# Attention stage of a trunk layer: 20 of 32 maximum shifts on GpSimd, and another order of the stage's works

## The chip, the cores and the metric

The kernel runs on one core of one Trainium2 chip. A core has five engines with a queue each, and each queue is worked off in order: PE (TensorE, matmuls; PEld is its weight load, which overlaps the matmuls), DVE (VectorE), ACT (ScalarE), POOL (GpSimd) and SP (SyncE, which here only issues DMAs). The metric is the time of one execution on the device in microseconds (us); less is better. Line numbers (L1123) are those of the kernel's file.

## The reference

One layer of a transformer trunk is computed for 128 context tokens and 512 latent tokens, with shared weights: a normalised and modulated projection `w_in`, attention beside a short gated convolution, an output projection, and a convolutional feed-forward part. The change lies in the attention, of which this is the core:

```python
q = rms_norm(q.reshape(B, N, N_HEADS, HEAD_DIM), p["q_norm"])       # 16 heads of 64
k = rms_norm(k.reshape(B, N, N_KV_HEADS, HEAD_DIM), p["k_norm"])    # 4 key heads
...
s = jnp.einsum('bqkgd,btkd->bkgqt', qblk, k).astype(jnp.float32) * scale
p = jax.nn.softmax(s, axis=-1).astype(v.dtype)
return jnp.einsum('bkgqt,btkd->bqkgd', p, v)
```

Context tokens attend to 128 keys without positions; latent tokens are rotated by two-dimensional positions and attend to 640 keys, of which 128 come from a cache.

## The kernel before, in words

**Values in two parts.** fp32 values are split into a high part (fp32r, by a copy on ACT) and a low part (value minus high part, a subtraction on DVE or POOL), and each product is three matmuls: high·high, low·high, high·low.

**The stage.** The attention stage begins when the projections of keys and values are done and ends before the attention's output projection (L235 to L237). It has 4 key heads g; for each it goes through 5 tiles t of 128 query tokens (tile 0 is the context). Each tile holds four query heads in two pairs. The 36 steps are numbered n = 9g + i: i = 0 is the context tile with both pairs at once, and i = 1 to 8 are tiles 1 to 4 with one pair each. These last are the 32 *blocks*; each treats two heads, h = 0 and h = 1.

**Before a block: a query tile.** `q{g}{t}.0` to `.3` are four quarters of its projection on PE (L709, 6 matmuls each). DVE rotates (`rot`: L849 and L850, into the tiles X and QF), DVE or POOL adds the two (`add`, L870), ACT squares (L872), DVE sums (L874), POOL takes the power -1/2 (`factor`, L877), POOL or DVE multiplies by it (`norm`, L892). PE turns the tile over (`turn`, L1034), and ACT and DVE split it (`hi`, `lo`: L1036, L1038). The key tiles go a similar way (`k{t}`: L849, L850, L870, L877, L882, L921, L927, L930). The values are scaled to an fp16 pair (`v scale`, L975; `v hi`, L981; `v lo`, L984).

**A block n.** `s{n}`: PE computes the scores of both heads (L1073, 12 matmuls), each head into one of three PSUM areas of two banks. `max{n}.h`: DVE takes the negated maximum over 640 keys (L1120). `shift{n}`: for h = 1 alone a constant is added to it (L1123, one number per partition). `exp{n}.h`: ACT (L1128), with the sum accumulated by a second instruction. `P1`: ACT rounds to fp16 (L1134). `P2`: the rest, again fp16; for h = 0 always on DVE (L1141), for h = 1 by L1139 on POOL or DVE. `T{n}.h`: SP issues a transposing DMA (L1145). `pv{n}`: PE multiplies with the values (L1162, L1170). Then `R`, `O`, `AH`, `AL` (L1182 to L1192) scale and split the output.

**Two ways for P2 of the second head.** Where `POOL_WAY` has a 1 for a block, the exponential goes to a buffer E in SBUF and POOL computes P2 from it; the score's PSUM area is free after the exponential. Where it has a 0, the exponential stays in PSUM and DVE computes P2. Before, blocks 28, 34 and 35 have a 0.

**What sets the order.** Nothing is scheduled in the stage while the kernel runs or is built: `PLAN` is a list of 944 items, each the number of a work, a letter (a or b: on which of its possible engines it is done) and digits (which free buffer or PSUM area it takes). `follow(PLAN)` issues them in that order. So each engine's queue holds its works in the order of the list, and a work waits there for its inputs, and for the last users of the buffers that it takes. Loads of weights (`load`) and their splits (`hi 10` to `hi 18`, `lo 10` to `lo 18`: L826, L831, two halves of 512 columns for each low part) are works of the list as well. A weight's low half that is not ready holds the projection quarters that use it.

The lines of a work that can be done by two engines look like this, here the addition of a query tile:

```python
last = also(work(f"{name} add", "POOL", lambda: add(G), [rot], orooms + [zt]), "DVE", lambda: add(V))
```

Of the kernel before, what the change touches and what calls it, by code (L numbers as in the profile page):

```python
# [18 lines left out]
ALU = mybir.AluOpType  # L19
# [31 lines left out]
67a0 44a0 12a00 203a 24a1 137a 34a2 68a 25a 13a 0a 32a11 131a 2a1 69a 11a 26a 6a 3a 41a 33b 70a 14a1 35a 51a2 4a 1a3 79a1 53a4  # L51
71a0 15a 21a 80a 36a 5b0 31a 72a2 81a 45a 52a3 7a 16a 37b1 82a 22a12 92a2 46a 85a1 73a 8a0 23b 83a10 17a2 54a3 9a 86a 132a 38a1
10a 27a3 42a01 18a0 39a 93a 55a 19a 43a 40a 28a4 74a 60b2 94a 29a 59b3 95a 87a 75b 20a 105a3 98a0 84a 30a 76a1 106a 88a 77a0 99a
78a 107a 100a 58b4 56a0 47b4 65a 347a2 57a 134b 61a 96a22 48a1 63a 348a 108a 97a 49a 118a0 349a 101a 109a01 119a 133b 50a 89a2
102a1 120a 62a 90a1 209a 111a2 351a1 91a 110a 121a 112a 138a 66a 113a 359a10 352a 124a1 103a2 114a 122a10 204a 353a5 365a 140b
115a4 135a0 116a3 366a 104a 367a0 139b 136a 117a 350a 360a 368a0 373a20 123a 275a 125a 361a 64a 126a 141a 362a4 379a 205b 142a
380a 371a 363a 381a1 354a1 369a 143a2 364a0 382a2 374a 391a10 355a2 144a0 356a 383a 375a 151a0 370a1 145a 397a 357a 152a 376a1
146a 398a 385a 384a2 392a 399a0 153a 377a 147a 393a 154a 358a 206b 405a02 394a3 378a3 155a01 400a4 395a 127a 148a1 157a2 411a
401a 149a0 128a3 372a0 396a4 129a1 412a 158a 413a1 130a 159a 406a 414a0 423a12 403a 402a5 150a 407a 415a 164a1 429a 408a2 165a
156a 430a 281a 409a 431a0 166a 416a0 160a 424a 432a1 167a 417a 425a 433a 437a02 168a20 426a3 435a 386a 170a1 443a 169a 410a1  # L60
444a 427a 177a1 387a2 445a1 388a 178a 438a 389a 428a2 446a4 455a12 390a 171a 439a 447a 404a0 456a 440a0 434a3 449a 457a 441a
172a 418a 461a 458a2 173a 161a2 442a4 419a1 179a 459a 162a2 180a 163a 462a 420a 463a0 469a10 448a5 181a10 464a3 467a 182a 487a2
470a 183a0 421a 465a 190a1 460a0 488a 471a 191a 475a 472a1 192a 422a 210a 184a 466a1 174a0 473a 193a 185a 175a3 489a 176a 476a
186a 194a02 450a0 211a 436a 212a 477a1 474a4 490a 195a 478a0 481a 499a10 196a2 907a 479a 451a1 197a 207a1 491a4 505a 276a 208a
198a 506a 480a5 452a 507a0 492a 213a 199a 500a 453a 513a20 508a2 493a2 454a 278b 501a 468a0 514a 509a 502a3 519a 515a 214a 503a
277b 510a3 516a1 482a 520a 215a2 521a1 517a 187a3 504a0 483a0 511a 525a 531a02 188a1 484a 522a0 189a 518a1 200a3 216a1 523a 537a
485a 494a1 201a0 486a 538a 217a 223a0 495a2 202a 524a4 218a 539a0 496a 224a 532a 497a 219a 540a4 545a12 498a 533a 911a 541a
220a1 551a 534a2 225a 221a2 552a 226a 535a 542a5 553a1 546a 554a3 563a02 227a11 547a 555a 536a2 222a 548a1 557a 512a1 569a 229a0
228a 570a 549a 571a0 526a 556a0 564a 572a0 577a12 543a 230a 527a0 573a 565a 528a 550a3 236a0 583a 529a 566a4 231a 237a 575a 584a
578a 585a1 238a 574a1 567a 232a 586a2 239a 530a 579a 587a 595a20 240a02 568a4 580a3 589a 544a1 242a2 601a 241a 602a 596a 558a  # L70
603a0 588a2 581a 597a 233a0 243a 609a01 234a3 607a 244a 559a1 582a5 235a 604a1 560a 249a0 610a 245a 561a 598a0 250a 562a 605a
611a 599a 246a1 251a 247a1 615a 600a0 612a4 627a2 616a 248a 617a1 252a 628a 606a3 618a2 590a1 621a 613a 255a1 619a 629a 256a
576a 253a20 614a2 257a 254b 639a10 591a2 620a5 630a 631a3 592a 258a 262a0 640a 593a 263a 594a 641a 645a 264a 282a 646a 632a 265a
647a0 633a1 283a 279a1 266a11 284b 642a0 280a 648a1 643a 653a20 267a 915a 268a0 651a 908a 644a4 269a 649a 608a0 654a 659a 655a
622a 270a 909a 650a0 656a4 259a3 660a 271a 661a1 285a 657a 910b 260a0 286a 665a 623a0 658a3 261a 662a2 272a2 624a 671a21 287a0
625a 663a 288a2 626a 273a2 289a 634a1 919a 677a 290a 664a2 295a0 678a 635a2 672a 679a0 291a 296a 274a 673a 636a 685a10 637a 683a
674a3 638a 297a 691a 680a0 298a 681a 692a 675a 693a1 292a1 299a21 676a5 694a1 703a20 686a 300a 301a1 293a3 302a 666a0 695a 687a
682a1 709a 688a4 697a 294a 652a 710a 303a 704a 696a2 711a0 689a 308a1 667a0 304a 705a 668a 717a01 690a3 669a 715a 712a2 670a
# [10 lines left out]
880a0 885a 934a 840a 856a0 841a 895a 886a5 896a 842a 935a2 897a 890a 898a1 936a 891a 899a 937a 892a4 901a 900a2 938a 943a 893a  # L89
939a 894a4 940a 870a 888a1 871a2 872a 902a 873a 874a 941a 903a1 904a 942a 905a 906a  # L90
"""
POOL_WAY = "11111111111111111111111101111100"


def rope_tables():
# [17 lines left out]
def trunk_layer(ctx, tc, x_prompt, x_sample, cache_k, cache_v, c, c_ctx, w_ada, b_ada, g_pre1, g_post1, g_pre2,  # L113
# [597 lines left out]
    SHIFT = 15  # L711
# [35 lines left out]
    with tc.tile_pool(name="att", bufs=1) as at:  # L747
# [305 lines left out]
        for n, (g, t, pi) in enumerate(steps):  # L1053
# [52 lines left out]
            else:  # L1106
                pts[n], exs = [], []
                for h in hs:
# [16 lines left out]
                    if h:  # L1125
                        mx = work(f"shift{n}", "DVE", shifted, [mx])
# [1398 lines left out]
```

## Time and profile before

| | us |
|---|---|
| median of three runs (lowest, highest) | 1075.21 (1074.77, 1075.44) |
| the profiled execution's own time | 1074.79 |
| its span | 1073.0 |
| of it the attention stage, about | 55 to 229 |

The granted clock of TensorE is full (0.999) all through. A row of a timeline or of the chain gives the start and the duration in us, the engine, the line, the operation, out<-in by names, and in brackets how long the engine had been idle and what released it. A row of groups gives the count, the busy time in us and the mean of one in ns, then the idle time ahead of them. Rows of windows give the busy time of each engine within a stretch. A busy PE is not a PE at its peak: matmuls are pipelined and their ends modelled.

### The profile page before, as it was taken

The numbers are of one execution on the slowest core, as the hardware profiler recorded it, in microseconds if no ns is written. First come the engines' busy times: TensorE is split into PE (matmuls) and PEld (weight loads), VectorE is DVE, ScalarE is ACT, GpSimd is POOL, SyncE is SP. The second block draws the span as 40 slices with busy tenths as digits, with TensorE's granted clock in tenths as the row PEclk, the third lists the DMA queues.
The fourth block names the chain that finished last, engine by engine and source line by source line (L and its number), as shares of the span: only waits on it lengthen the run. The fifth ranks groups of instructions, "written<-read, shape, count | busy, mean of one in ns | idle before, by whom it ended". The sixth has DMA issues, their size and how long they took to land.

```text
span 1073.0 us, 20652 instructions
## 1 busy us (share of the span) xinstructions
PE 1056.8 (98%) x8216; PEld 995.4 (93%) x8216; DVE 899.9 (84%) x1379; ACT 598.4 (56%) x1057; POOL 133.1 (12%) x162
## 2 busy tenths in 40 slices
PE   8999999999999999999999999999999999999997
PEld 6788898899999999999998789999999999999996
DVE  5699999865498999896599678889999988989897
ACT  5478999942344544445322366645555555546673
POOL 1087676500000000000000020000000000000001
PEclk9999999999999999999999999999999999999999
DMA  9829999962244333223668634434544534436873
GB/s 320 256 82 175 190 168 187 191 147 60 75 123 124 93 103 94 79 79 99 189 188 253 198 131 129 121 116 136 166 131 152 150 122 131 152 116 219 277 275 115
DMA packets 243197, 164.02 MB, mean 153 GB/s; under 512 B 94874, under 2 KB 216214, under 8 KB 243102
## 3 DMA queue, kind: packets, MB, share of 16 engines
q1 hardware_dynamic: 242990, 162.68, 55.5%
q8 instruction: 64, 1.05, 0.4%
q14 instruction: 31, 0.25, 0.1%
q10 hardware_dynamic: 112, 0.04, 0.0%
HBM read 123.31 MB, written 17.36 MB: 131 GB/s over the span
## 4 chain that ended last, share of the span: by engine, by line
PE 90%; DVE 3%; ACT 2%; DMA 1%; POOL 1%; issue 1%; SPq 1%; DVEq 0%; ACTq 0%; POOLq 0%
PE b L1274 47%; PE b L235 10%; PE b L237 10%; PE b L236 9%; PE s L709 4%; PE s L1073 2%; PE s L1170 2%; PE s L235 1%; PE s L237 1%; PE s L1162 1%; PE s L478 1%; DVE marks L1120 1%; PE s L236 1%; PE b L1900 1%; ACT P L1134 1%
## 5 line engine op out<-in xcount | busy, mean ns | idle before, releaser
L1274 PE MATMUL b<-ZBr,whi 128*128 128x320 f32 x688 | 152.1, 309 | 0.0
L1274 PE MATMUL b<-MT,whi 128*128 128x320 f32 x608 | 134.4, 309 | 0.0
L1274 PEld LDWEIGHTS b<-ZBr,whi 128*128 128x128 f32 x688 | 114.9, 188 | 0.1
L1274 PE MATMUL b<-ZBr,wlo 128*128 128x320 f32 x344 | 106.1, 308 | 0.0
L1274 PEld LDWEIGHTS b<-MT,whi 128*128 128x128 f32 x608 | 101.7, 188 | 0.0
L1274 PE MATMUL b<-MT,wlo 128*128 128x320 f32 x304 | 94.0, 309 | 0.0
L1261 ACT ACTIVATE whi<-SUM 128x1024 fp32r<-128x1024 f32 x40 | 42.2, 1055 | 78.3 <-DVE SUM L1813 75.7
L1843 DVE SCALAR_TENSOR_TENSOR Y<-C,cffn,Y 128x642 f32<-128x642 f32 x88 | 77.9, 886 | 0.9
L1261 ACT ACTIVATE whi<-WB 128x1024 fp32r<-128x1024 f32 x38 | 40.2, 1058 | 55.5 <-DVE WB L1368 55.5
L1274 PE MATMUL b<-ZBT,whi 128*128 128x320 f32 x320 | 71.0, 308 | 0.0
L1274 PE MATMUL b<-UL,whi 128*128 128x320 f32 x228 | 70.8, 311 | 0.0
L1274 PE MATMUL b<-UH,wlo 128*128 128x320 f32 x228 | 70.1, 307 | 0.0
L1274 PE MATMUL b<-UH,whi 128*128 128x320 f32 x228 | 69.7, 306 | 0.0
L1282 ACT ACTIVATE p<-b 128x320 f32<-128x320 f32 x78 | 34.1, 437 | 55.3 <-PE b L1274 53.5
L1274 PEld LDWEIGHTS b<-ZBr,wlo 128*128 128x128 f32 x344 | 64.6, 188 | 0.0
L1265 DVE TENSOR_TENSOR wlo<-raw,whi 128x1024 fp32r<-128x1024 f32 (+1 forms) x51 | 50.4, 1020 | 13.4 <-ACT whi L1261 13.4
L1274 PEld LDWEIGHTS b<-MT,wlo 128*128 128x128 f32 x304 | 57.1, 188 | 0.0
L1274 PEld LDWEIGHTS b<-ZBT,whi 128*128 128x128 f32 x320 | 54.2, 188 | 1.6
L1120 DVE TENSOR_REDUCE marks<-s 128x1 f32<-128x640 f32 x64 | 52.1, 817 | 4.0 <-PE s L1073 3.8
L1265 DVE TENSOR_TENSOR wlo<-WB,whi 128x1024 fp32r<-128x1024 f32 x38 | 46.5, 1224 | 8.8 <-ACT whi L1261 8.7
L2355 POOL TENSOR_TENSOR ssqs<-ssqs 128x1 f32<-128x1 f32 x4 | 1.4, 356 | 412.9 <-ACT GJ L2349 412.9
L1261 ACT ACTIVATE whi<-raw 128x1024 fp32r<-128x1024 f32 (+1 forms) x51 | 43.5, 892 | 15.4 <-DMA raw<-in_w_o_dram 12.5
(477 smaller groups left out, 3348.1 us busy)
## 6 DMA issues: line engine op xcount, KB each, us to landing
raw<-in_w_in_dram SPq DMA_DIRECT2D x48, 512.0 KB
RAW<-in_w_up_dram SPq DMA_DIRECT2D x40, 512.0 KB
raw<-in_w_down_dram SPq DMA_DIRECT2D x22, 512.0 KB
GA<-in_w_ada_dram SPq DMA_DIRECT2D x16, 512.0 KB
actd<-Y SPq DMA_DIRECT2D x18, 321.0 KB
actl<-ACTb SPq DMA_DIRECT2D x18, 321.0 KB
A<-actl SPq DMA_DIRECT2D x9, 642.0 KB
A<-actd SPq DMA_DIRECT2D x9, 642.0 KB
```

What stands on the lines that cost most here:

```text
L235: PE.matmul(out, ah, bh, start=start, stop=False)
L236: PE.matmul(out, ah, bl, start=False, stop=False)
L237: PE.matmul(out, al, bh, start=False, stop=stop)
L709: PE.matmul(out, a, b, start=start and n == 0, stop=stop and n == 2, skip_group_check=True)
L1073: PE.matmul(o[h], q_of(hl, i, rows), kk[kx][rows, g, ks], start=m == 0, stop=m == 2, tile_position=(64 * h, 0), skip_group_check=True)
L1120: V.tensor_reduce(out=mk[:, h:h + 1], in_=s_of(), axis=AX.X, op=ALU.max, negate=True)
L1170: PE.matmul(p[64 * h:64 * h + 64, i * 128:i * 128 + 128], VH[:, w, s, vc_], src, start=k == 0 and m == 0, stop=k == ks[-1][0] and m == 2, ...
L1261: S.activation(to[0], raw, AF.Copy)
L1265: V.tensor_tensor(out=lo, in0=raw, in1=hi.bitcast(F32), op=ALU.subtract)
L1274: PE.matmul(out, p[:, ws], q[:, k, :], start=start and k == 0 and n == 0, stop=stop and k == 3 and n == 2, skip_group_check=True)
L1282: S.activation(t, pair[j][b], AF.Copy)
L1843: V.scalar_tensor_tensor(out=y, in0=crows(j)[i][:, d:d + NACT], scalar=cffn[:, 44 * d + o:44 * d + o + 1], in1=y, op0=ALU.mult, op1=ALU.add)
```

## The change

1. The work `shift{n}` gets a second way: the same addition by POOL (letter b in the list).
2. The list is another one. In it 20 of the 32 shifts are done by POOL (blocks 1 to 6, 8, 10, 11, 13, 15, 17, 19, 20, 24, 25, 26, 28, 30 and 31), the other 12 by DVE as before.
3. `POOL_WAY` has a 0 for block 35 alone: P2 of the second heads of blocks 28 and 34 moves from DVE to POOL.
4. The letters of other works differ as well. Counted over both lists: additions of query tiles on DVE 2 before and 8 now (of 16), their norms on DVE 1 and 7 (of 20), additions of key tiles on DVE 2 and 1 (of 4), scalings of the values on DVE 3 and 1 (of 3), low parts of the values on DVE 3 and 2 (of 3), halves of weights' low parts on DVE 5 and 6 (of 18).
5. The order of all works, and the digits of the buffers, are new. Outside the stage the order of every engine is what it was.

```diff
 PLAN = """
-67a0 44a0 12a00 203a 24a1 137a 34a2 68a 25a 13a 0a 32a11 131a 2a1 69a 11a 26a 6a 3a 41a 33b 70a 14a1 35a 51a2 4a 1a3 79a1 53a4
...
+67a0 11a 32a00 137a 44a0 203a 2a1 22a11 68a 33a 14a2 131a 51a2 12a32 69a 41a 21a 3a 13a 70a 31a 15a 24a1 1a4 34a2 4a 79a1 25a 0a
...
 """
-POOL_WAY = "11111111111111111111111101111100"
+POOL_WAY = "11111111111111111111111111111110"
...
-                    def shifted(mk=mk):
-                        V.tensor_scalar(out=mk[:, 1:2], in0=mk[:, 1:2], scalar1=SHIFT * math.log(2), scalar2=None, op0=ALU.add)
+                    def shifted(eng, mk=mk):
+                        eng.tensor_scalar(out=mk[:, 1:2], in0=mk[:, 1:2], scalar1=SHIFT * math.log(2), scalar2=None, op0=ALU.add)
...
-                        mx = work(f"shift{n}", "DVE", shifted, [mx])
+                        mx = also(work(f"shift{n}", "DVE", lambda f=shifted: f(V), [mx]), "POOL", lambda f=shifted: f(G))
```

**Place A, the beginning of the stage, POOL's queue** up to the norm of the query tile q03 (the last row of each piece, L892 on QF0). QF0 to QF2 are query tiles in work, X0 to X2 the second halves of rotations, wlo the low parts of weights, rq and rk the factors. Before:

```order
L870 TENSOR_TENSOR QF1_763<-QF1_763,X0_759 128x256
L892 TENSOR_TENSOR QF1_763<-QF1_763,rq_769 128x256
L877 TENSOR_TENSOR rq_769<-ssqs_771,mhalf_81 128x4
L831 TENSOR_TENSOR wlo_102_908<-raw_95_797,whi_101_907 128x512
L870 TENSOR_TENSOR QF2_764<-QF2_764,X2_761 128x256
L892 TENSOR_TENSOR QF2_764<-QF2_764,rq_769 128x256
L831 TENSOR_TENSOR wlo_102_908<-raw_95_797,whi_101_907 128x512
L870 TENSOR_TENSOR QF0_762<-QF0_762,X1_760 128x256
L877 TENSOR_TENSOR rq_769<-ssqs_771,mhalf_81 128x4
L892 TENSOR_TENSOR QF0_762<-QF0_762,rq_769 128x256
```

Now:

```order
L975 TENSOR_TENSOR P0_745<-VV_172,vrow_773 128x512
L975 TENSOR_TENSOR P2_747<-VV_172,vrow_773 128x512
L892 TENSOR_TENSOR QF1_763<-QF1_763,rq_769 128x256
L877 TENSOR_TENSOR rq_769<-ssqs_771,mhalf_81 128x4
L984 TENSOR_TENSOR VV_172<-P2_747,VV_172 128x512
L831 TENSOR_TENSOR wlo_103_928<-raw_95_797,whi_102_927 128x512
L870 TENSOR_TENSOR QF1_763<-QF1_763,X2_761 128x256
L1123 TENSOR_SCALAR marks_772<-marks_772 128x1
L892 TENSOR_TENSOR QF2_764<-QF2_764,rq_769 128x256
L877 TENSOR_TENSOR rq_769<-ssqs_771,mhalf_81 128x4
L831 TENSOR_TENSOR wlo_105_1059<-raw_96_799,whi_104_1058 128x512
L892 TENSOR_TENSOR QF0_762<-QF0_762,rq_769 128x256
```

The three additions of q01 to q03 (L870) have left POOL for DVE; two scalings and one low part of the values (L975, L984), the shift of block 1 (L1123) and the addition and factor of q04 have come in ahead of this norm. On PE, the turn of q03 stood directly behind the scores of block 1; now three projection quarters (q10.0, q10.1, q10.2), the turn of q02 and the scores of block 2 stand between them.

**Place B, blocks 11 to 14, POOL's queue.** Here L1139 is P2 of blocks 11, 12, 13 and 14 in turn (from the buffers E1, E0, E1, E0 or the other way round). Before:

```order
L1139 TENSOR_TENSOR P0_745<-E1_744,P0_745 128x640
L877 TENSOR_TENSOR rq_769<-ssqs_771,mhalf_81 128x4
L892 TENSOR_TENSOR QF2_764<-QF2_764,rq_769 128x256
L1139 TENSOR_TENSOR P4_749<-E0_743,P4_749 128x640
L1139 TENSOR_TENSOR P3_748<-E1_744,P3_748 128x640
L870 TENSOR_TENSOR QF1_763<-QF1_763,X1_760 128x256
L1139 TENSOR_TENSOR P0_745<-E0_743,P0_745 128x640
```

Now:

```order
L877 TENSOR_TENSOR rq_769<-ssqs_771,mhalf_81 128x4
L1139 TENSOR_TENSOR P3_748<-E0_743,P3_748 128x640
L1139 TENSOR_TENSOR P2_747<-E1_744,P2_747 128x640
L1123 TENSOR_SCALAR marks_772<-marks_772 128x1
L1139 TENSOR_TENSOR P0_745<-E0_743,P0_745 128x640
L870 TENSOR_TENSOR QF2_764<-QF2_764,X1_760 128x256
L1139 TENSOR_TENSOR P3_748<-E1_744,P3_748 128x640
```

The shift of block 13 stands directly behind P2 of block 12, and the norm of q20 (L892) has left this queue.

**The same place, DVE's queue**, from the maximum of block 13's second head (the first row of each piece) to the rotation of the query tile q21 (L849). Before:

```order
L1120 TENSOR_REDUCE marks_772<-s2_103_933 128x1
L1123 TENSOR_SCALAR marks_772<-marks_772 128x1
L1141 SCALAR_TENSOR_TENSOR P2_747<-s2_99_880,P2_747 128x640
L1120 TENSOR_REDUCE marks_772<-s2_100_898 128x1
L849 TENSOR_TENSOR X1_760<-s1_94_787,tabq_477 128x256
L850 TENSOR_TENSOR QF1_763<-s1_94_787,tabq_477 128x256
L1038 TENSOR_TENSOR QT2_767<-s1_98_840,QT2_767 128x256
```

Now:

```order
L1120 TENSOR_REDUCE marks_772<-s2_100_888 128x1
L1141 SCALAR_TENSOR_TENSOR P4_749<-s2_101_905,P4_749 128x640
L1147 RECIPROCAL marks_772<-marks_772 128x2
L1038 TENSOR_TENSOR QT2_767<-s1_94_787,QT2_767 128x256
L1120 TENSOR_REDUCE marks_772<-s2_99_879 128x1
L849 TENSOR_TENSOR X1_760<-s1_98_840,tabq_477 128x256
```

The shift is gone from DVE, and the low part of q20 (L1038) stands three works earlier, ahead of the maximum of the first head.

On PE, between the scores of blocks 31 and 32 stood `pv27` and the turn of q34; now the turn of q34, `pv27` and `pv28` stand there. The last works of PE in the stage were gate1 1.1, pv33, pv34, pv35 and two gate quarters; now they are gate1 1.0, gate1 1.1, pv34, pv35 and the same two quarters (the gate quarters are matmuls of L709 that wait for nothing there).

More of the change, by code (lines that the diff above doesn't have):

```diff
@@ L55 @@
[L55 to L66, printed above, removed]
```

66 lines of the change are left out of this document (39 added, 27 removed).

## The prediction

> **What bounds the kernel now.** I read the page first: the busy shares and the chain that ended last. Then I cut the span into stretches and asked within the attention stage, the only place that is changed, who idles and for whom.
>
> ```profile
> PE 1056.8 (98%) x8216; PEld 995.4 (93%) x8216; DVE 899.9 (84%) x1379; ACT 598.4 (56%) x1057; POOL 133.1 (12%) x162
> PE 90%; DVE 3%; ACT 2%; DMA 1%; POOL 1%; issue 1%; SPq 1%; DVEq 0%; ACTq 0%; POOLq 0%
> ```
>
> TensorE carries the kernel; nine tenths of the chain are matmuls. A change that leaves them alone can win only what PE waits. The stage in three windows (columns: busy time of PE, PEld, DVE, ACT, POOL):
>
> ```profile
> 55.00:92.00 37.00, 34.81 (x334) 31.81 (x334) 35.46 (x86) 29.49 (x69) 33.68 (x33) 1.00 0.48 106
> 92.00:200.00 108.00, 106.38 (x1548) 95.71 (x1543) 98.83 (x221) 99.36 (x233) 71.19 (x69) 1.00 1.11 184
> 200.00:229.00 29.00, 28.01 (x421) 26.02 (x421) 18.52 (x37) 21.48 (x48) 5.18 (x4) 1.00 0.95 161
> ```
>
> PE idles 2.19, 1.62 and 0.99 us: 4.8 us of 174. That is the ceiling of the gain that the rows show, 0.45% of the kernel; only a little may hide in modelled ends of matmuls. In the first window DVE is busy for 96% and POOL for 91%; there these two set the pace. In the second, DVE and ACT are busy for 92% each, and POOL has room. Whom PE waits for in the stage (total us, times, longest):
>
> ```profile
> PE s L1034 <- POOL QF L892: 1.8, 2, 1.1
> PE s L1073 <- DVE P L1141: 0.8, 2, 0.6
> PE s L1162 <- DVE QT L1038: 0.5, 1, 0.5
> PE s L1170 <- DMA PT<-P: 0.4, 1, 0.4
> ```
>
> None of them names the shift or the maximum. The largest is the turn of a query tile that waits for its norm on POOL, and both cases lie in the first window.
>
> **The change: busy time.** The rows that price it (count, busy us, mean ns):
>
> ```profile
> L1139 POOL TENSOR_TENSOR P<-E,P 128x640 f16<-128x640 f32 x29 | 40.8, 1408 | 30.3 <-ACT P L1134 30.2
> L877 POOL TENSOR_TENSOR rq<-ssqs,mhalf 128x4 f32<-128x4 f32 x20 | 21.3, 1067 | 3.9 <-DVE ssqs L874 3.8
> L831 POOL TENSOR_TENSOR wlo<-raw,whi 128x512 fp32r<-128x512 f32 x13 | 17.8, 1379 | 5.4 <-ACT whi L826 5.4
> L892 POOL TENSOR_TENSOR QF<-QF,rq 128x256 f32<-128x256 f32 x19 | 11.6, 613 | 1.3
> L870 POOL TENSOR_TENSOR QF<-QF,X 128x256 f32<-128x256 f32 x14 | 11.5, 821 | 3.0 <-DVE marks L1147 2.5 <-DVE QF L850 0.5
> L882 POOL TENSOR_TENSOR PT<-P,rk 128x512 f32<-128x512 f32 x2 | 2.3, 1173 | 0.0
> L870 POOL TENSOR_TENSOR P<-P,X 128x256 f32<-128x256 f32 x2 | 1.5, 738 | 3.0 <-DVE P L850 3.0
> L1711 POOL TENSOR_SCALAR ssq<-ssq x5: 207/209/623, 611.7 to 614.5; 128x1 f32<-128x1 f32 x5
> L1139 DVE TENSOR_TENSOR P<-s,P 128x640 f16<-128x640 f32 x3 | 2.5, 822 | 0.7 <-ACT P L1134 0.7
> L984 DVE TENSOR_TENSOR VV<-P,VV 128x512 f16<-128x512 f32 x3 | 2.4, 786 | 0.0
> L975 DVE TENSOR_TENSOR P<-VV,vrow 128x512 f32<-128x512 f32 x3 | 2.0, 686 | 0.0
> L870 DVE TENSOR_TENSOR QF<-QF,X 128x256 f32<-128x256 f32 x2 | 1.1, 528 | 0.0
> L892 DVE TENSOR_TENSOR QF<-QF,rq 128x256 f32<-128x256 f32 x1 | 0.4, 421 | 0.0
> L831 DVE TENSOR_TENSOR wlo<-raw,whi 128x512 fp32r<-128x512 f32 x5 | 3.9, 794 | 0.8 <-ACT whi L826 0.8
> ```
>
> - DVE loses 20 shifts (0.15 each by the row at 127.94 below: 3.0), two P2 (1.6), two scalings (1.4), a low part of the values (0.8) and a key addition (0.4, taken as a query tile's, 0.53 at most): -7.2. It gains six additions (6 x 0.528 = 3.2), six norms (2.5) and half a weight (0.8): +6.5. The balance is -0.7 us. The relief that the shifts bring is spent again on the query tiles.
> - POOL gains 20 shifts, two P2 (2.8), a key addition (0.7), two scalings (as L882, 2.3) and a low part of the values (as L831, 1.4), and loses six additions (4.9), six norms (3.7) and half a weight (1.4): -2.8 without the shifts. The trace has no shift on POOL. L1711 is the same operation on the same shape: 0.21, and once, after a long idle time, 0.62. I take 0.21, so 4.2 in all: POOL +1.4; with 0.62 it would be +9.6.
> - ACT and PE do the same instructions, SP issues the same 68 transposes and 10 loads. None of the balances is on PE's path; what counts is who is late where.
>
> **Term 1, the beginning (place A).** Rows of POOL and PE there:
>
> ```profile
> 57.40 0.74 POOL L870 TENSOR_TENSOR P<-P,X 128x256 f32<-128x256 f32 x1 [2.55 <-DVE P L850]
> 78.07 0.61 POOL L892 TENSOR_TENSOR QF<-QF,rq 128x256 f32<-128x256 f32 x1
> 78.73 0.44 PE L1034 MATMUL s<-ident,QF 128*128 128x128 f32 x2 [0.74 <-POOL QF L892]
> 90.86 0.44 PE L1034 MATMUL s<-ident,QF 128*128 128x128 f32 x2 [1.09 <-POOL QF L892]
> 96.71 1.08 PE s L1073 x12
> 98.16 0.84 PE s L1170 x30
> 149.61 4.44 PE s L709 x36
> ```
>
> Before, POOL worked from 57.40 through to the norm of q03, which ended at 78.68; PE had waited 0.74 for it. Ahead of that norm now come in two scalings (2.35), a low part of the values (1.38), a key addition (0.74), a shift (0.21), the addition and factor of q04 (0.82, 1.07) and a half of lo 11 (1.38): 7.9. Three additions (2.46) and a half of lo 10 (1.38) go: 3.8. The norm comes 4.1 later. PE's turn of q03 comes later as well, by three quarters (4.44 / 36 x 6 = 0.74 each), a block's scores (1.08) and a turn (0.15): 3.4. The wait grows from 0.74 to 0.74 + 4.1 - 3.4 = 1.4. The low half that q10.2 needs ends one norm earlier, and q10.2 stands about a quarter earlier: the same wait, not a second one. The 1.09 at 90.86 was the turn of q04 behind its norm on POOL. That norm is now on DVE (0.42), and POOL has seven works (6.3 us) from q03's norm through q10's, while PE has eight quarters, three scores and a `pv` (some 9.8 us): no wait. Term 1: +0.7 - 1.1 = -0.4. With the scalings at DVE's price (0.69) it would be -1.4; with POOL's new works 15% dearer (1.2 of 7.9), +0.8.
>
> **Term 2, two waits that lose their cause (place B and block 32).**
>
> ```profile
> 200.64 0.65 PE L1073 MATMUL s<-KH,QT 64*128 64x320 f32 x2 [0.58 <-DVE P L1141]
> 130.73 0.44 PE L1162 MATMUL s<-ident,marks 128*64 128x128 f32 x4 [0.46 <-DVE QT L1038]
> ```
>
> The first is block 32's scores, which take the area that P2 of block 30's first head leaves. That P2 now stands a low part (0.42) later on DVE and is rid of a shift (0.15) ahead of it, but one more `pv` (0.84 by the row at 98.16) now stands on PE between the two scores: 0.58 + 0.27 - 0.84 is nothing, so -0.58. The second is `pv10`, in whose bank q20 was turned: the low part of q20 stands three works earlier on DVE, ahead of a maximum: -0.46. Either may also be passed on to the next work of PE; then it is 0.
>
> **Term 3, the shift in the chain from scores to scores.** The next block needs an area that the exponential of h = 1 frees. Block 13 to block 14, before:
>
> ```profile
> 125.89 0.42 PE L1073 MATMUL s<-KH,QT 64*128 64x320 f32 x2
> 126.50 1.41 POOL L1139 TENSOR_TENSOR P<-E,P 128x640 f16<-128x640 f32 x1
> 127.08 0.82 DVE L1120 TENSOR_REDUCE marks<-s 128x1 f32<-128x640 f32 x1 [0.71 <-PE s L1073]
> 127.94 0.15 DVE L1123 TENSOR_SCALAR marks<-marks 128x1 f32<-128x1 f32 x1
> 128.19 0.80 ACT L1128 ACTIVATE E<-s,marks 128x640 f32<-128x640 f32 x1
> 129.01 0.53 PE L1073 MATMUL s<-KH,QT 64*128 64x320 f32 x2 [0.17 <-DVE P L1141]
> ```
>
> From the maximum's end (127.90) to the exponential it was 0.29. By POOL: 0.05 to hand over (as from POOL to PE at 78.68, 78.73), 0.21, 0.05 again: 0.31, if POOL is free. So a shift costs the chain next to nothing and saves it nothing. It decides where PE comes back within some 3.4 us, which among POOL's blocks are 1, 2, 13 and 31 by the order; I take 0.1 for each: +0.4, between 0 and what the first rival says.
>
> **Term 4, DVE and POOL at the same time.** POOL's additions of query tiles take 0.821 in the mean, those of key tiles, of the same size, 0.738. A long one lies beside DVE instructions with two inputs from SBUF:
>
> ```profile
> 112.01 1.82 DVE L831 TENSOR_TENSOR wlo<-raw,whi 128x512 fp32r<-128x512 f32 x2
> 112.24 1.04 POOL L870 TENSOR_TENSOR QF<-QF,X 128x256 f32<-128x256 f32 x1 [0.18 <-DVE QF L850]
> ```
>
> Here POOL lost 0.30 against the key tiles' 0.738, and DVE 0.23 (1.82 for two against 2 x 0.794). Such DVE instructions (additions, norms, scalings, low parts) become nine more: 6 + 6 + 1 - 1 - 2 - 1. At 0.53 each that is 4.8 us of the two engines if every one meets POOL, 3.2 us at POOL's two thirds of the time. Of such a delay I let a sixth reach PE, since neither engine is waited for often: +0.5, between 0 and 1.6.
>
> The last wait, 0.4 for the transposes of block 35, I leave: that block's scores stand earlier on PE, but its last transpose is now issued behind the other head's. The sum: -0.4 - 0.58 - 0.46 + 0.4 + 0.5 = -0.54. Against the profiled execution's own 1074.79 that is 1074.25; the median of the runs stands 0.42 higher, so I forecast 1074.7. The rivals' times are given against the median.
>
> **The rivals.** *No change beyond 0.2%* (2.15 us, about what a measurement of this kernel can tell) is what the sum says.
>
> *Faster.* The waits of the first window go altogether (1.83), with the two of term 2 (1.04) and one of the small ones (0.4), and DVE's relief in the second window, where DVE is at 92%, costs nothing elsewhere: -3.3, 1071.9. Against it: the new order has PE, DVE and POOL just as full at the beginning.
>
> *Slower: POOL's queue holds the exponentials.* A shift waits behind whatever POOL does. At place B it stands behind P2 of block 12, which ended at 127.91, while the maximum ended at 127.90. Any lateness of that P2 (its input comes from ACT, and POOL waited 30.2 us for that in the stage) now delays the exponential, ACT behind it, and block 14's scores, one for one, up to 1.41. Nine of the 20 shifts stand directly behind a P2. If three of them lose 1.2 each, the sum turns into +3.1: 1078.3. From -0.54, two such places that lose 1.4 bring it past +0.2%.
>
> *Slower: exclusion.* The long additions above show that the two engines hinder each other. The Trainium skill (SBUF — State Buffer, section "SBUF: two separate sides") says that a DVE instruction with two SBUF inputs and a GpSimd instruction that reads SBUF exclude each other for the whole instruction, whoever starts first. As a mechanism of this kernel: if all of term 4's 3.2 us reached PE, the sum were -1.04 + 3.2 = +2.2, 1077.4. Under that rule the one norm on DVE, in a window in which POOL was busy for 91%, should have stretched, and its 0.421 is shorter than the additions' 0.528 on tiles of the same size; so the trace agrees in part.
>
> **How the numbers follow.** Forecast (within 0.2%) 0.48; faster rival 0.26; POOL's queue 0.20; exclusion 0.06. So faster 0.26, same 0.48, slower 0.26. The range, 1071.8 to 1078.3, reaches to both outer cases; for the forecast alone it is 1073.1 to 1077.3.
>
> **What would show it.** Right: PE's wait for POOL's norms falls from 1.8 to about 1.4 in one piece near 81; the waits at block 32's scores and `pv10` are gone; L1123 on POOL takes about 0.21; ACT's wait for L1123 is no longer than before; DVE's busy time in the stage within 1 us of 152.8. Wrong: several PE waits at L1073 for ACT with POOL's L1123 behind L1139; POOL's L1123 above 0.4; L870 and L892 stretched on DVE; or PE idle in the stage well under 3 us.

## The measured result, and the profile after

The changed kernel takes 1079.2 us (median of 6 runs, 1078.39 to 1083.18), the kernel before, with as many runs, 1074.99. The ratio is 1.0044, its 95% interval 1.0033 to 1.0055: slower by 4.7 us, by the interval 3.5 to 5.9 (the two medians lie 4.2 apart; where a loss is priced by ratios below, the text says so). The forecast was 1074.7, and the range ended at 1078.3. The profiled execution took 1079.36 with a span of 1077.6, 4.6 more than before's 1073.0, so it shows the whole loss. The stage itself, from PE's first matmul of L709 to the end of its last one there, takes 175.9 us in it (56.93 to 232.83) and took 171.6 before (56.76 to 228.35): 4.3 longer, nearly all of the 4.6.

The page's busy line after the change, and the stage in the three windows of the prediction (busy time of PE, PEld, DVE, ACT, POOL, then the granted clock, the DMA engines' share and GB/s):

```profile
PE 1060.0 (98%) x8216; PEld 997.1 (93%) x8216; DVE 900.4 (84%) x1366; ACT 600.3 (56%) x1057; POOL 135.6 (13%) x175
```

```profile
55.00:92.00 37.00, 34.92 (x309) 31.38 (x308) 35.29 (x80) 28.41 (x65) 33.01 (x34) 1.00 0.44 97
92.00:200.00 108.00, 106.70 (x1548) 95.84 (x1547) 98.76 (x212) 100.80 (x234) 72.82 (x79) 1.00 1.04 181
200.00:229.00 29.00, 26.50 (x372) 24.11 (x372) 18.29 (x36) 21.00 (x46) 6.76 (x6) 0.94 1.06 183
```

PE idles 2.08, 1.30 and 2.50 us, where it had idled 2.19, 1.62 and 0.99. The first two windows are no worse. The third is worse by 1.5, and it has something that the profile before did not have in the stage: a granted clock of 0.94. PE also does the same number of instructions with 3.2 us more busy time (1060.0 against 1056.8). Whom PE waits for in the stage (total us, times, longest):

```profile
PE s L1073 <- ACT E L1128: 1.3, 2, 1.2
PE s L1170 <- DMA PT<-P: 1.3, 1, 1.3
PE s L709 <- POOL wlo L831: 1.0, 1, 1.0
PE s L1034 <- POOL QF L892: 0.4, 1, 0.4
```

The first is new, the second was 0.4 before, and both lie in the last window. Cut into pieces of 2 us, that place reads:

```profile
210.00:212.00 2.00, 0.84 (x10) 0.75 (x11) 1.49 (x3) 2.00 (x5) 0.00 (x0) 1.00 1.19 255
212.00:214.00 2.00, 0.91 (x11) 0.55 (x8) 1.31 (x5) 1.96 (x5) 1.40 (x1) 0.89 1.03 167
214.00:216.00 2.00, 1.84 (x34) 1.83 (x35) 1.43 (x3) 1.33 (x3) 0.57 (x1) 0.50 1.13 226
216.00:218.00 2.00, 2.00 (x40) 1.91 (x39) 0.00 (x0) 0.37 (x2) 0.83 (x1) 0.75 0.91 108
```

PE stands still for more than half of 210 to 214. The clock is 0.50 from 213.6 to 217.0; the 0.89 and 0.75 are means of pieces that this stretch covers in part. The lowered clock costs up to 2 x (0.11 + 0.50 + 0.25) = 1.7 us; PE is idle for the first 0.6 us of the stretch, so 1.4 falls where it works. The rows of ACT and PE at this place say what it waited for:

```profile
209.72 0.70 ACT L1134 ACTIVATE P<-s 128x640 f16<-128x640 f32 x1 [1.66 <-DMA PT<-P]
211.25 0.55 PE L1073 MATMUL s<-KH,QT 64*128 64x320 f32 x2 [1.16 <-ACT E L1128]
214.16 1.81 PE L1170 MATMUL s<-PT,VV 128*64 128x128 f16 x30 [1.26 <-DMA PT<-P]
```

ACT's P1 of block 32's first head wants one of the five P buffers, and a transpose still reads it. Queued behind that P1 on ACT is the exponential of block 33, which frees what the scores of block 34 need: PE waits 1.16. The transposed values of block 31 then wait 1.26 for their transpose. The queue of which the prediction had only counted the works is SP's, which issues the transposes. Its rows at the end of the stage, before (start, us, operation, how many):

```profile
189.38 1.38 SPq L1145 DMA_TRANSPOSE PT<-P  x1
191.70 0.37 SPq L217 DMA_DIRECT2D raw<-in_w_att_out_dram  x1
193.42 2.13 SPq L1145 DMA_TRANSPOSE PT<-P  x1
195.65 1.22 SPq L217 DMA_DIRECT2D raw<-in_w_att_out_dram  x1
197.24 6.95 SPq L1145 DMA_TRANSPOSE PT<-P  x4
```

and after:

```profile
194.44 2.38 SPq L1145 DMA_TRANSPOSE PT<-P  x1
196.92 0.53 SPq L217 DMA_DIRECT2D raw<-in_w_att_out_dram  x1
197.55 4.01 SPq L1145 DMA_TRANSPOSE PT<-P  x2
201.62 0.66 SPq L217 DMA_DIRECT2D raw<-in_w_att_out_dram  x1
202.38 5.79 SPq L1145 DMA_TRANSPOSE PT<-P  x2
```

Among the transposes stand two loads of output weights, 512 KB each. They are not works of the list, and so not under the sentence of "What sets the order" that nothing is scheduled in the stage: the kernel's text has them behind the stage, and by the rows they come into SP's queue soon after their buffers become free. Before, both stood ahead of block 29's transposes, and the first fell into a gap, between 189.38 + 1.38 and 193.42. After, one stands ahead of block 29's two transposes and one ahead of block 30's. The last two of these took 5.79 together (2.73 and 2.89 and a short gap), where a transpose's median is 1.49. The buffer of a load is a weight's, and its last reader here is a low half on POOL. It ended at 194.85 before and at 199.14 after, behind P2 of block 29 and the shift of block 30:

```profile
192.32 2.53 POOL L831 TENSOR_TENSOR wlo<-raw,whi 128x512 fp32r<-128x512 f32 x2
```

```profile
196.06 1.41 POOL L1139 TENSOR_TENSOR P<-E,P 128x640 f16<-128x640 f32 x1
197.56 0.22 POOL L1123 TENSOR_SCALAR marks<-marks 128x1 f32<-128x1 f32 x1
197.86 1.28 POOL L831 TENSOR_TENSOR wlo<-raw,whi 128x512 fp32r<-128x512 f32 x1
```

That POOL's low half is what moved the second load is read from these rows alone; no run moves only the low half, and none puts only the two P2 of blocks 28 and 34 back on DVE. What the loads cost at their places is tried below.

### The profile page after: what moved, and what is told of

The parts are those of the page before. It is cut to its first block, busy times and chain, and to the rows that moved or that the text cites. A ratio compares the mean times of both kernels' runs of the same rounds, so it can differ in the third digit from the quotient of the medians.

```text
span 1077.6 us, 20634 instructions
## 1 busy us (share of the span) xinstructions
PE 1060.0 (98%) x8216; PEld 997.1 (93%) x8216; DVE 900.4 (84%) x1366; ACT 600.3 (56%) x1057; POOL 135.6 (13%) x175
## 4 chain that ended last, share of the span: by engine, by line
PE 86%; DVE 4%; ACT 3%; DMA 2%; issue 2%; POOL 2%; SPq 0%; DVEq 0%; ACTq 0%; POOLq 0%
PE b L1274 47%; PE b L235 10%; PE b L237 10%; PE b L236 9%; PE s L709 3%; DMA PT<-P 1%; PE s L1073 1%; PE s L1170 1%; ACT P L1134 1%; PE b L1900 1%; PE s L478 1%; DMA araw<-in_w_ada_dram 1%; PE s L1162 1%; ACT E L1128 1%; DVE P L1141 1%
```

## Experiments

Two theories stood at first. A: the new order loses the time, at the end of the stage through the loads among the transposes, and perhaps at its beginning. B: the shift on POOL is itself what costs. Each ratio is to the runs of the kernel before on the same chip, with its 95% interval.

**The new order, all shifts on DVE.** In the list the letter b of the 20 shifts becomes a. The line with the shift of block 1 (item 366):

```diff
-89a3 120a 90a1 66b 348a 138a 121a 91a 349a 359a21 64a 122a12 133b 365a 123a 135a0 209a 124a2 360a 351a4 366b 101a 136a 367a0
+89a3 120a 90a1 66b 348a 138a 121a 91a 349a 359a21 64a 122a12 133b 365a 123a 135a0 209a 124a2 360a 351a4 366a 101a 136a 367a0
...
```

> The new order with all 20 shifts of the new kernel back on DVE at their places in the order; nothing else changed. Theory A (the order lost the time, at the tail and at the front, and a shift on GpSimd costs nothing): the time stays at 1078 to 1080, and the 1.2 us pause of TensorE before the scores of block 34 and the 1.3 us pause before the transposed values (line 1170) near 213 stay. Theory B (the shift on GpSimd is what costs, behind P2 in GpSimd's queue or by contention on DVE): about 1075 or below, and these pauses go.

Measured: 1082.02 us, 1.0068 (1.0055 to 1.0080), slower still than the changed kernel. Taking the shift back from POOL mends nothing; theory B as it stood falls. But neither did the time stay, as A had it: ACT's wait for the shifts rose from 2.6 us to 7.1, and one pause of 2.7 before the transposed values took the place of the two.

**The order of before, the 20 shifts on POOL.** The two edits of lines 1122 to 1126 as in the change, and the letter b for the shifts of the same 20 blocks, in the old list. The line with the shift of block 1:

```diff
-115a4 135a0 116a3 366a 104a 367a0 139b 136a 117a 350a 360a 368a0 373a20 123a 275a 125a 361a 64a 126a 141a 362a4 379a 205b 142a
+115a4 135a0 116a3 366b 104a 367a0 139b 136a 117a 350a 360a 368a0 373a20 123a 275a 125a 361a 64a 126a 141a 362a4 379a 205b 142a
...
-                    def shifted(mk=mk):
-                        V.tensor_scalar(out=mk[:, 1:2], in0=mk[:, 1:2], scalar1=SHIFT * math.log(2), scalar2=None, op0=ALU.add)
+                    def shifted(eng, mk=mk):
+                        eng.tensor_scalar(out=mk[:, 1:2], in0=mk[:, 1:2], scalar1=SHIFT * math.log(2), scalar2=None, op0=ALU.add)
...
-                        mx = work(f"shift{n}", "DVE", shifted, [mx])
+                        mx = also(work(f"shift{n}", "DVE", lambda f=shifted: f(V), [mx]), "POOL", lambda f=shifted: f(G))
```

> The order of before, with the 20 shifts of the new kernel issued on GpSimd and nothing else changed. Theory A: 1074.5 to 1076, within 1 us of before, since a shift of 0.22 on GpSimd replaces one of 0.15 on DVE; by the chains on which the score waits (some 20 hops of 0.1 to 0.2 longer, few of them on the path) at most +1. Theory B: 1077 to 1080.

Measured: 1084.28 us, 1.0091 (1.0077 to 1.0104): neither theory's number, and the dearest kernel of all. The shift itself takes 0.22 here too; what is dear is its place in POOL's queue. The example of block 31 in that kernel's timeline:

```profile
206.20 0.82 DVE L1120 TENSOR_REDUCE marks<-s 128x1 f32<-128x640 f32 x1 [0.27 <-PE s L1073]
207.30 1.40 POOL L1139 TENSOR_TENSOR P<-E,P 128x640 f16<-128x640 f32 x1 [2.57 <-ACT P L1134]
208.78 0.21 POOL L1123 TENSOR_SCALAR marks<-marks 128x1 f32<-128x1 f32 x1
209.02 0.80 ACT L1128 ACTIVATE E<-s,marks 128x640 f32<-128x640 f32 x1 [1.80 <-POOL marks L1123]
209.96 0.41 PE L1073 MATMUL s<-KH,QT 64*128 64x320 f32 x1 [1.74 <-ACT E L1128]
```

The maximum was done at 207.02. POOL was then waiting for ACT with P2 of block 30 at the head of its queue, and the shift stood behind it, so it began 1.76 later; ACT waited 1.80 for the shift and PE 1.74 for ACT. This is the prediction's first slower rival, in full. Who waited for the shift's line, in all of this kernel (us, times):

```profile
ACT E L1128: 13.7, 18
ACT s L1128: 1.7, 2
```

and in the changed kernel:

```profile
ACT E L1128: 2.3, 7
...
ACT s L1128: 0.3, 1
```

From the end of each maximum to the start of its shift I summed, over the 20 shifts on POOL, 17.4 us in the old order and 5.8 in the new one. The new order has made room for the shift on POOL. That this is also why its list doesn't suit DVE is likely, and not shown.

**The same, with 16 of these shifts one place up in POOL's queue.** In the old list, the P2, add, factor, norm or low half that stood directly ahead of the shift is put directly behind it. For block 31, the P2 of block 30 (821) and the shift (832):

```diff
...
-831a 821a 344a0 832b 815a 833a0
+831a 344a0 832b 821a 815a 833a0
...
```

> The order of before with the 20 shifts on GpSimd (which gave 1084.3), and 16 of these shifts moved one place up in GpSimd's queue, ahead of the P2, add, factor, norm or low half behind which they stood. If the loss comes from the place in the queue (the shifts started 17.4 us in sum after their maxima ended, against 5.8 for the 20 in the new kernel): this sum falls below 7 and the time to 1075 to 1078, the rest being what GpSimd now waits for a maximum. If it comes from the engine itself (its semaphores, or DVE held up by GpSimd's accesses): 1082 or above.

Measured: 1077.85 us, 1.0026 (1.0016 to 1.0036); the sum of the shifts' delays fell to 4.9. Of the 9.7 us that the shifts had cost in the old order, 6.8 come back with the places in the queue. The 2.9 that remain over the kernel before are no proof of a price of the engine, since the works put behind the shifts became later.

**The new order, both loads behind the last transpose.** One line in the loop that works off the list:

```diff
-            w.done = True
+            w.done = w.name != "T35.1" or bool((state.update(limit=22), fetch(22)))
```

> The new order, with the two loads of output weights that SP issued among the last transposes (at 196.92 and 201.62 in the new kernel) put behind the last transpose; the same bytes, the same other order. Theory A1 (the second load, which stands just ahead of the two transposes of block 30, stretches them from 1.4 to 2.7 and 2.9 and so holds the P buffer that ACT waits for at 209.7): both transposes near 1.5 to 2, ACT's wait of 1.7 gone, TensorE's pauses of 1.2 and 1.3 gone and the lowered clock behind them with it: 1075 to 1076.5. Rival A2 (the transposes are late for another reason, their order or P2's, and are stretched by turns anyway): 1078 to 1079.5, under 1 us gained.

Measured: 1075.61 us, 1.0009 (1.0000 to 1.0018). The end of the stage is mended: by the ratios 3.8 us of the 4.7 come back (1.0044 to 1.0009) by moving two DMA issues. The last window and the four transposes of blocks 29 and 30:

```profile
200.00:229.00 29.00, 28.84 (x441) 26.31 (x439) 18.88 (x38) 22.28 (x50) 6.51 (x6) 1.00 1.09 187
```

```profile
197.23 6.46 SPq L1145 DMA_TRANSPOSE PT<-P  x4
```

PE idles 0.16 there instead of 2.50, and its clock stays at 1.00. These two, 2.34 and 1.4 to 1.7, are together 3.7 to 4.0, where the stage is 4.0 shorter (171.9 against 175.9). The four transposes took 6.46 from the first to the end of the last, against 10.62 with both loads among them (197.55 to 208.17).

**The new order, only the second load behind the last transpose.** As above, with the first load issued behind the transpose T28.1, its place in the changed kernel.

```diff
-POOL_WAY = "11111111111111111111111111111110"
+POOL_WAY = "11111111111111111111111111111110"; LOAD_AT = {'T28.1': 21, 'T35.1': 22}
...
-            w.done = True
+            w.done = w.name not in LOAD_AT or bool((state.update(limit=LOAD_AT[w.name]), fetch(LOAD_AT[w.name])))
```

> The new order, with only the second of the two loads (201.62, between the transposes of block 29 and of block 30) put behind the last transpose; the first stays between the second transpose of block 28 and those of block 29. If the second load alone loses the tail: 1075 to 1076.5, as with both late. If the first counts too (the transposes behind it were issued 0.3 to 1.5 us later in the new kernel than with both loads late): 1076.5 to 1078, with part of the pauses before block 34 left.

Measured: 1076.03 us, 1.0013 (1.0004 to 1.0022). The second load alone is nearly all of it, 3.3 us by the ratios. The first still counts in the queue, though hardly in the median: the four transposes took 8.23. The traced execution took 1078.53, 2.5 above the median, and in it PE waits 1.4 for a transpose; so the first load can cost something as well.

```profile
198.69 8.23 SPq L1145 DMA_TRANSPOSE PT<-P  x4
```

**The new order, an eighth of the second load in its place,** the other seven eighths behind the last transpose.

```diff
+POOL_WAY = "11111111111111111111111111111110"; LOAD_AT = {'T28.1': 21, 'T29.0': 22, 'T35.1': 23}
...
+    part, EIGHTH = [], {'T29.0': (0, 1), 'T35.1': (1, 8)}
...
-            nc.sync.dma_start(raw[:, :nk * n].rearrange("p (k c) -> p k c", c=n),
-                              w[k0 * 128:(k0 + nk) * 128, c0:c0 + n].rearrange("(k p) c -> p k c", p=128))
+            (part.append if len(state["raw"]) == 21 else lambda f: f(0, nk))(lambda a, b, raw=raw, w=w, k0=k0, c0=c0, n=n: nc.sync.dma_start(
+                raw[:, a * n:b * n].rearrange("p (k c) -> p k c", c=n), w[(k0 + a) * 128:(k0 + b) * 128, c0:c0 + n].rearrange("(k p) c -> p k c", p=128)))
...
-            w.done = True
+            w.done = w.name not in LOAD_AT or bool((state.update(limit=min(LOAD_AT[w.name], 22)), fetch(22), part and part[0](*EIGHTH[w.name])))
```

> The new order and both loads in their places of the new kernel, but of the second only an eighth (64 KB) stands between the transposes of block 29 and of block 30; the other seven eighths (448 KB) follow behind the last transpose. If it is the bytes ahead of the transposes that stretch them: block 30's two transposes near 1.5 to 2.1 instead of 2.7 and 2.9, and the time of the second load put behind the last transpose, 1075.3 to 1077. If it is the load as such (a second kind of DMA among the transposes in SP's queue): both stay above 2.5, and 1078 to 1080.

Measured: 1076.74 us, 1.0017 (1.0008 to 1.0026). The instruction is there, the bytes are not, and most of the loss is gone: block 30's transposes took 3.88 together instead of 5.79. The traced execution took 1078.34, 1.6 above the median; its stage is 172.9, and PE waits 1.0 for a transpose in it.

```profile
198.01 3.82 SPq L1145 DMA_TRANSPOSE PT<-P  x2
201.88 0.79 SPq L217 DMA_DIRECT2D raw<-in_w_att_out_dram  x1
202.78 3.88 SPq L1145 DMA_TRANSPOSE PT<-P  x2
```

**The new order, both loads between the transposes of block 29 and those of block 30.** The same edit with

```diff
+POOL_WAY = "11111111111111111111111111111110"; LOAD_AT = {'T29.0': 22}
```

> The new order with both loads, 1 MB, between the transposes of block 29 and those of block 30: the cause doubled at that place. If the bytes ahead of block 30's transposes set the tail: their issue starts or lands 2 to 3 us later than in the new kernel, less the 0.3 to 1.5 that the transposes of block 29 gain, and the time goes to 1080 to 1083. If the tail only ever loses what one wait for a P buffer costs: 1078.5 to 1080, as in the new kernel.

Measured: 1079.30 us, 1.0043 (1.0029 to 1.0057): a miss for the theory of the place, which had 1080 to 1083. The rows offer a reason:

```profile
197.63 2.97 SPq L1145 DMA_TRANSPOSE PT<-P  x2
200.65 1.36 SPq L217 DMA_DIRECT2D raw<-in_w_att_out_dram  x2
202.12 6.18 SPq L1145 DMA_TRANSPOSE PT<-P  x2
```

Block 29's transposes are quick now and block 30's slower, and the four end after 10.67 (197.63 to 208.30), as with one load ahead of each pair. By these rows the end of the four depends on how many bytes stand anywhere ahead of it, and not on how many stand at one place. Five kernels of one order (the transposes and the stage are of one traced execution, whose own time follows; the last column is the median of all):

| loads among or just ahead of the four transposes | the four transposes, us | the stage, us | that execution, us | median, us |
|---|---|---|---|---|
| none | 6.46 | 171.9 | 1075.19 | 1075.61 |
| 512 KB | 8.23 | 173.7 | 1078.53 | 1076.03 |
| 576 KB | 8.65 | 172.9 | 1078.34 | 1076.74 |
| 1024 KB, one load ahead of each pair (changed kernel) | 10.62 | 175.9 | 1079.36 | 1079.2 |
| 1024 KB, both between the pairs | 10.67 | 174.0 | 1078.37 | 1079.30 |

Each load adds about 2.1 us to the queue, but the median rises little until the second. ACT was ready for its buffer at 208.06 (209.72 - 1.66) in the changed kernel, and went on at 209.72. So of the 4.2 us that the loads add there, about 2.5 would have been free for ACT, by these rows; with 512 and 576 KB ACT indeed waits for no transpose. PE's wait for the transposes themselves, 1.4 and 1.0 in these two traces, is not covered by that slack. The stages also show that part of the 1078.53 and 1078.34 was lost outside the stage. The execution of the last row took 0.9 less than the median and has a mean clock of 0.999; the other four have 0.997, as the changed kernel's traced one has, so its trace probably lacks a fall of the clock that they had.

**The kernel before, its second load where the new kernel has it,** behind the transpose T29.0, the first where it was: the same edit, in the old kernel, with

```diff
+POOL_WAY = "11111111111111111111111101111100"; LOAD_AT = {'T28.0': 21, 'T29.0': 22}
```

> The kernel before, with only the second of these loads moved three transposes on, to where the new kernel has it: between the transposes of block 29 and those of block 30. If the place of the load is what lost the tail (and not the new order's other places), TensorE pauses before the scores of block 34 or 35 and the transposed values: 1076.5 to 1079. If the old order has the slack to take it (its first transpose of block 30 is issued at 200.91 against 202.38): 1074.5 to 1075.5, and then the place alone is not enough, it needs the new order's later transposes too.

Measured: 1075.93 us, 1.0010 (1.0001 to 1.0019), between the two forecasts. The place alone is not enough for the 4.7. A reason that the rows offer, and no run tests: in the old order the transposes of block 29 begin at 197.14 in this kernel, about when they do in the new one, but the first load lies before them in the gap, and only one load is left to be made up for.

**The kernel before, both loads behind the last transpose.**

```diff
-            w.done = True
+            w.done = w.name != "T35.0" or bool((state.update(limit=22), fetch(22)))
```

> The kernel before, with the two loads that stand among its last transposes (191.70 and 195.65) put behind the last transpose. If loads among the transposes are what stretches them and the tail waits on them, the tail of before gains too, though less, since nothing there waits for a P buffer: its last pause before the transposed values (0.6 near 224.7) and part of the 0.8 before the scores of block 35 go: 1073.5 to 1074.8. Rival (the tail of before is set by ACT and DVE, not by the transposes): within 0.4 of before. If the loads are wanted soon after the stage, slower: 1076 and above.

Measured: 1075.23 us, 1.0001 (0.9992 to 1.0010): no change. The end of the old order doesn't wait on these loads, as the rival had it, and there is nothing to be won there.

**The new order, all shifts on DVE, both loads behind the last transpose.** The first experiment's letters and the line for `T35.1`.

> The new order with all shifts on DVE (which gave 1082.0) and with the two loads behind the last transpose. If the loads are the tail's loss there too (a pause of 2.7 before the transposed values): 1078 to 1079.5, and what is left over the new kernel with late loads (1075.6), some 3 us, is what the shift's places on DVE in this order cost. If the tail there waits for something else: 1081 or above.

Measured: 1078.44 us, 1.0031 (1.0019 to 1.0042). The loads cost 3.6 there (1082.02 - 1078.44; 4.0 by the ratios), and the remaining 2.8 over 1075.61 is what the new list loses when its shifts go back to DVE.

**The beginning: the values' works back on DVE.** In the new list, two scalings and a low half of the values go from POOL to DVE at the same places:

```diff
-47b4 76a4 19a 108a 59a0 77a0 20a 48a0 111a1 118a1 78a 49a 60a2 109a00 347a0 50a 56a4 88a 61a 112a 119a 65a 110b 113a 57a 62a 63a
-89a3 120a 90a1 66b 348a 138a 121a 91a 349a 359a21 64a 122a12 133b 365a 123a 135a0 209a 124a2 360a 351a4 366b 101a 136a 367a0
+47b4 76a4 19a 108a 59b0 77a0 20a 48a0 111a1 118a1 78a 49a 60b2 109a00 347a0 50a 56a4 88a 61a 112a 119a 65a 110b 113a 57a 62a 63a
+89a3 120a 90a1 66a 348a 138a 121a 91a 349a 359a21 64a 122a12 133b 365a 123a 135a0 209a 124a2 360a 351a4 366b 101a 136a 367a0
```

> The new order, with the two scalings of the values (v scale 1 and 2) and their low half (v lo 2), which the new order gives to GpSimd at 71.97 to 77.78 (3.7 us), back on DVE (0.7 each, as before) at the same places. Theory A (GpSimd's queue is what is late at the front: TensorE's wait for a weight's low half, 1.0, and for the norms near 81 and 83): these waits fall by 1 to 2 together, 1077.0 to 1078.5. Rival (DVE, with 2.1 us more in 65 to 78, is as late, or the front's gain is lost again at the tail): 1079 or above.

Measured: 1080.26 us, 1.0051 (1.0039 to 1.0064), no gain. The pause before the low half is gone, and others have come (both loads are still among the transposes here, where PE waits 2.1 at one place, so the time holds the end of the stage as well):

```profile
PE s L1073 <- DVE QT L1038: 1.5, 2, 1.2
PE s L1034 <- POOL QF L892: 0.7, 2, 0.4
```

**The beginning, and the loads late: one work of POOL later.** Both loads behind the last transpose, and the item 66b (the low half of the values) from ahead of the weight's low half to behind the shift of block 2 (380b).

```diff
-89a3 120a 90a1 66b 348a 138a 121a 91a 349a 359a21 64a 122a12 133b 365a 123a 135a0 209a 124a2 360a 351a4 366b 101a 136a 367a0
-125a 352a 126a 102a1 368a1 139a 373a10 353a5 103a2 140b 350a 361a 104a 379a 362a3 114a 141a 275a 374a 204a 380b 369a 115a1 363a
+89a3 120a 90a1 348a 138a 121a 91a 349a 359a21 64a 122a12 133b 365a 123a 135a0 209a 124a2 360a 351a4 366b 101a 136a 367a0
+125a 352a 126a 102a1 368a1 139a 373a10 353a5 103a2 140b 350a 361a 104a 379a 362a3 114a 141a 275a 374a 204a 380b 66b 369a 115a1 363a
```

> The new order with both loads behind the last transpose (which gave 1075.6), and on GpSimd the low half of the values (v lo 2, 1.2 us) moved from ahead of the weight's low half that TensorE waits for at 78.16 to behind the shift of block 2; it is wanted only by the values of block 0 near 87. If GpSimd's queue at the front is what keeps the new order behind before, once the tail is mended: the 1.0 pause at 78.16 and 0.3 to 0.5 of those near 81 and 83 go, 1073.8 to 1075.0, not slower than before. If DVE and the turns set the front anyway, the pauses only move: 1075.3 to 1076.2.

Measured: 1076.70 us, 1.0017 (1.0008 to 1.0025), slower by some 1 us than with the late loads alone, though the intervals overlap; the stage is 173.4 in the trace against 171.9. The pause before the weight's low half went, and the norm came later:

```profile
PE s L1034 <- POOL QF L892: 1.5, 2, 1.2
```

Twice the rival's mechanism was right, the second time at 0.5 us more than it had: in the first window POOL and DVE are both full, and a work taken from one place there is missed at another. No version beat the kernel before; the nearest are the old order with its loads late and the new one with its loads late.

## Why the prediction was wrong, point by point

- **The step that failed** is the one on SP: "SP issues the same 68 transposes and 10 loads. None of the balances is on PE's path", and with it "The last wait, 0.4 for the transposes of block 35, I leave". The works were counted and their places were not compared; the two loads that are not in the list are among the ten. So SP's part of the sum was put at nothing for no better reason than equal counts. The term that was missing is the second load's move past block 29's transposes. Together with the first load it made ACT wait 1.66 and PE 1.16 + 1.26, and put up to 1.7 of lowered clock on top; the runs price both loads at 3.8 us of the 4.7, and the second alone at 3.3. In the old order the same move of the second load costs only some 1.0 (1.0010), so it takes something else of the new order too, which no run singles out. The profile before had a hint in SP issuing four transposes in 6.95 without a gap; the DMA share is no sign of the loss, since it is 1.09 in the last window with the loads late, where nothing is lost.
- **The ceiling** of 4.8 us of visible idle time bounded the gain only. A forecast that close to zero needed a floor for the loss as well, and the range's upper end came from the shift's rival alone.
- **Term 1** came out about right in its sum, in part by chance, and with another name on it. Forecast was one wait of 1.4 near 81 and none at 90.86. Measured are two, of 0.96 and 0.40, and none at 90.86:

```profile
79.51 0.39 PE L709 MATMUL s<-wlo,UH 128*128 128x256 f32 x1 [0.96 <-POOL wlo L831]
84.03 0.33 PE L1034 MATMUL s<-ident,QF 128*128 128x128 f32 x1 [0.40 <-POOL QF L892]
131.38 0.44 PE L1162 MATMUL s<-ident,marks 128*64 128x128 f32 x4
202.58 0.42 PE L1073 MATMUL s<-KH,QT 64*128 64x320 f32 x2
```

  The longer one is for a weight's low half, not for the norm; the prediction had called it "the same wait, not a second one". Both sides of its difference were too small: the norm of q03 ends 5.3 later (83.98 against 78.68) where 4.1 was forecast, and PE is ready for its turn 5.6 later (83.63 against 77.99) where 3.4 was. PE's idle time in the window fell by 0.11, against -0.4 forecast, within its own range.
- **Term 2** was right: `pv10` (131.38) and the scores of block 32 (202.58) carry no wait any more.
- **Term 3** was right in its mechanism, the shift's 0.22 for 0.15, and too dark in its size: ACT waits 2.6 us for the shifts instead of 5.1, and with the loads late PE waits 0.2 at L1073 for ACT, where +0.4 was forecast.
- **Term 4** was not borne out in the means. POOL's additions of query tiles became shorter, 0.73 in the mean instead of 0.82, with nine more such DVE instructions beside POOL. By the rule of the Trainium skill (SBUF — State Buffer, section "SBUF: two separate sides") they should have been held up more. But single places do look like the rival of exclusion, and one lies where PE waits its 0.96: a low half of the values on DVE that starts at 76.83, beside the one on POOL, takes 1.50 (two of the three took 0.68 before), and POOL's low half of the weight behind it 1.71, where 1.28 is the median. These 0.43 are nearly half of PE's wait. No run takes such a pair apart.

```profile
76.62 1.16 POOL L984 TENSOR_TENSOR VV<-P,VV 128x512 f16<-128x512 f32 x1
77.74 1.71 POOL L831 TENSOR_TENSOR wlo<-raw,whi 128x512 fp32r<-128x512 f32 x1
L870 POOL TENSOR_TENSOR QF<-QF,X 128x256 f32<-128x256 f32 x8 | 5.8, 731 | 1.0 <-DVE QF L850 0.5 <-DVE marks L1147 0.4
L1123 POOL TENSOR_SCALAR marks<-marks 128x1 f32<-128x1 f32 x20 | 4.4, 218 | 6.5 <-DVE marks L1120 5.4
```

- **The rival of POOL's queue** has the right mechanism for the old order (9.7 us) and not for the new kernel, whose order leaves the shifts 5.8 us late in sum. The sign that was to show it, PE waits at L1073 for ACT, did come (1.3), but there ACT waited for a transpose and not for a shift. That the time came out near its 1078.3 is chance: the loss lies elsewhere.
- **What stays open.** With its loads late, the new order is still 1.0 us behind (the interval begins at none), though PE's visible idle time in the three windows is 2.09 + 1.30 + 0.16 = 3.55 against 4.80 before. In the traces its stage is only 0.3 longer (171.9 against 171.6). The waits that are gone may have come back inside PE's busy time, since the ends of matmuls are modelled; no run settles where.

## What to carry to other kernels

When an order is changed, look through every queue place by place, the DMA queue too, with the transfers that the new order doesn't list but whose buffers it frees; equal counts say nothing. A long transfer is free in a gap of a queue and dear ahead of a transfer that somebody waits for, and its price only shows once the slack behind it is used up. Choosing an engine for a small work on a chain means choosing its place in that engine's queue: one order with the shift on the engine it was made for lost 9.7 us on the other, at nearly the same price of the instruction (0.22 for 0.15).

## What the runs showed of the hardware that was not expected

- A transpose of 128 x 1280 f16 takes SP 1.3 to 1.5 us to issue at its fastest (median 1.49), and 2.7 and 2.9 behind a load of 512 KB on the same queue; some take 2.1 with no load directly ahead. 512 KB add 1.8 to 2.1 us to the four transposes of the table. The Trainium skill (DMA: Bandwidth & Descriptors, section "Queues, rings and completion order") says that what SP issues goes through one row of rings, whose descriptors each DMA engine consumes in ring order; that transposes behind a load take longer agrees with it.
- The granted clock fell to 0.50 in the changed kernel inside the second of two pauses of PE of 1.16 and 1.26 us (210.09 to 214.16), and stayed there for 3.4 us; with the values' works on DVE it fell for as long (216.5 to 219.9) behind one pause of 2.1 us (213.04 to 215.16). It did not fall where PE stood still once for 2.7 us (the new order with its shifts on DVE), nor in the trace with pauses of 0.4 and 1.5 (both loads between the pairs). The Trainium skill (TensorE: Matmul & The Clock Gate, section "Why this matters for your kernels") asks for no gaps over about 3 us; here shorter ones were enough. What decides is not shown.
